# Turning rows into columns by VectorE squares and small transfers instead of TensorE transposes, in a fused GLA and ConvFFN layer

## The chip, the cores and the metric

The kernel runs on one core of a Trainium2 chip. The metric is the time of one execution on the device in microseconds (us). Before the change it was 2142.13 us, the median of three runs (2141.64 to 2144.13). Engines are called as in the profile: PE is TensorE (matmul), PEld its weight load, DVE VectorE, ACT ScalarE, POOL GpSimd, and SP SyncE, which here issues every transfer.

## The reference: what is computed

One layer of a decoder with 2048 tokens of width 1024: gated linear attention (GLA) with 4 heads, then a feed-forward network (FFN) with a causal convolution of width 3. Each of the two is modulated by a vector c, and followed by a residual and a layer norm:

```
def post_norm_residual(x, cs, w_mod, b_mod, ln_gain, ln_bias, sublayer):
    shift, scale, gate = jnp.split((cs @ w_mod + b_mod)[:, None, :], 3, axis=-1)
    y = sublayer(x * (1 + scale) + shift)
    return layer_norm(DN_ALPHA * x + (1 + gate) * y, ln_gain, ln_bias)

x = post_norm_residual(x, cs, mod_w[0, 0], mod_b[0, 0], ln_g[0, 0], ln_b[0, 0], gla)
x = post_norm_residual(x, cs, mod_w[0, 1], mod_b[0, 1], ln_g[0, 1], ln_b[0, 1], ffn)
```

The GLA part is `x @ w_in`, a chunked recurrence with a state per head, a norm per head, a gate, and `@ w_o`. The FFN part is `(silu(conv(u)) * g) @ w_down` with `u, g = split(h @ w_up)`, 2816 channels each. Everything is float32.

## The kernel before

**Number format.** A float32 matrix is split in two parts of PE's fast 32-bit format, high and low: ACT rounds (line 107) and DVE subtracts (line 110). A product is then three matmuls (`mm3`, lines 113 to 115). All matmuls of 512 columns come from there.

**The GLA part.** The tokens are worked on in four blocks of 512 (`tb` = 0 to 3, here the first to the fourth block). Each block goes through 32 units, a unit being one tile of weights of 24 matmuls. Weights come through `unit()`, which asks for the tile three units further on. The split weights are kept in HBM (`wq_d`) and come back from there as 1 MB loads (`hl<-wq_d`, line 136); in the third and fourth blocks all of them do. There are four buffers for them. What isn't a unit's own matmuls (the steps of the heads, the modulation, the gate of the FFN) is hung on unit numbers with `at_unit`, and done in `tick()` between two units. The instructions are then ordered on each engine by a scheduler, within what `order(later, earlier)` asks for. All DMAs leave from one queue on SP, in its order, and eight can be under way: a ninth waits for the first.

**Between GLA and FFN.** At the end of a block `ln1` normalises the rows `z` (128 tokens x 1024) and stores them in `zn_d`. The FFN needs them turned: channels on the partitions, tokens in a row. `ln1_out` does that: for each of 8 column tiles of 128 channels PE transposes four squares of 128x128 into a PSUM tile (line 844), DVE (line 849) or ACT (line 847) applies scale `A2` and shift `B2`, and the tile is stored in `xm2_d`. The second and third blocks do that directly from their rows `z`, behind the block's end. The first block does it in the third one's units 13 to 16, since `A2` and `B2` are not there earlier, with `z` loaded again from `zn_d`. The fourth block does it in the FFN's iterations 3 to 6.

**Also in the third block.** `gate_step` (eight steps, 512 KB load each into a tile of the `raw` pool, line 256; product and sum on DVE, lines 258 and 260) and `gate2` make `G2`, the gate of the FFN: two matmuls with ones (line 268), two additions on DVE (line 269) into `G2t`, stored to `G2_d` (line 888) and loaded later. At the block's end the rows `x` for the residual come in (`z<-in_x`, line 804), and the next block's columns of x (`xraw<-in_xT`, line 386).

**The FFN.** Two halves of 1024 tokens, 22 channel tiles each: 44 iterations. An iteration has seven products of 4 x 3 matmuls (Strassen-like combinations of four quarters, which `x_pre` prepares for the tokens from `xm2_d`), the convolution, and loads of the next pair of weights (`wu`, `wg`, lines 333 and 334). A stage of `hidden @ w_down` and the last norm follow.

Of the kernel before, what the change touches and what calls it, by code (L numbers as in the profile page):

```python
# [8 lines left out]
F32 = mybir.dt.float32  # L9
F32R = mybir.dt.float32r  # L10
U32 = mybir.dt.uint32
AF = mybir.ActivationFunctionType
# [4 lines left out]
P = 128  # L17
D = 1024
S = 2048
KT = D // P  # L20
# [18 lines left out]
def kernel(  # L39
# [46 lines left out]
    def raw_tile(name="raw"):  # L86
        return rawp.tile([P, 1024], F32, tag="raw", name=name)
# [24 lines left out]
    def mm3(po, a, b, first, last, resumed=False):  # L112
        nc.tensor.matmul(po, a[0], b[0], start=first, stop=False, skip_group_check=resumed)  # L113
        nc.tensor.matmul(po, a[0], b[1], start=False, stop=False, skip_group_check=resumed)  # L114
        return nc.tensor.matmul(po, a[1], b[0], start=False, stop=last, skip_group_check=resumed)  # L115
# [81 lines left out]
    ws_d = [dram.tile([P, 2, 512], F32, name=f"ws_d{j}") for j in range(NJ)]  # L197
    xt_d = [[[dram.tile([P, 1024], F32, name=f"xt_d{h}_{i}_{r}") for r in range(2)] for i in range(7)] for h in range(2)]
    wq_d = [dram.tile([P, 2, 1024], F32, name=f"wq_d{n}") for n in range(32)]
    xm2_d = [[dram.tile([P, 2, TB], F32, name=f"xm2_d{t}_{k}") for k in range(4)] for t in range(NTB)]  # L200
    G2_d = dram.tile([P, D], F32, name="G2_d")

# [160 lines left out]
    def at_unit(u, fn, *a):  # L363
        steps.setdefault(u, []).append((fn, a))
# [11 lines left out]
    if True:  # L376
# [288 lines left out]
        def gemm_f(xm):  # L665
            w = unit()
            wv = w.rearrange("p s (k c) -> p s k c", k=KT)
            po = psum("mm", 4)
            for kt in range(KT):
                mm3(po, (wv[:, 0, kt], wv[:, 1, kt]), (xm[kt][:, 0], xm[kt][:, 1]), kt == 0, kt == KT - 1)  # L670
            return po

        def gemm_q(xm, E, tick, pq=None):
# [159 lines left out]
        def ln1_out(tb, zs, prs, by_act=False):  # L833
            for pr in prs:
# [4 lines left out]
                for k in range(2):  # L839
# [9 lines left out]
                        nc.vector.tensor_scalar(xt, pt, A2[:, kt:kt + 1], B2[:, kt:kt + 1], op0=ALU.mult, op1=ALU.add)  # L849
                    store(xm2_d[tb][pr][:, k], xt)  # L850

        def normalise(z, after=None):
            st = smp.tile([P, 2, 6], F32, tag="bst", name="bst")
            for i in range(2):
                bn = nc.vector.bn_stats(st[:, i], z[:, i * 512:i * 512 + 512])
                if after is not None:
                    order(bn, after)
            mv = smp.tile([P, 2], F32, tag="mv", name="mv")
            nc.vector.bn_aggr(mv, st)
            rs = smp.tile([P, 2], F32, tag="rs", name="rs")  # L860
            rsqrt_eps(rs[:, 0:1], mv[:, 1:2])
            nc.gpsimd.tensor_scalar(rs[:, 1:2], mv[:, 0:1], rs[:, 0:1], -1.0, op0=ALU.mult, op1=ALU.mult)
            nc.scalar.activation(z, z, AF.Identity, bias=rs[:, 1:2], scale=rs[:, 0:1])
# [28 lines left out]
        for tb in range(NTB):  # L892
# [18 lines left out]
                        at_unit(b + 6 + n, mod_fin, 1, n // 4)  # L911
                at_unit(b + 22, mod2)
            if tb == 2:
                for pr in range(4):
                    at_unit(b + 13 + pr, ln1_out, 0, None, (pr,))
                for k in range(8):
                    at_unit(b + 14 + k, gate_step, 1, k, gs2)
                at_unit(b + 22, gate2)
# [32 lines left out]
                        Hs[h]["sr"].append(gemm_r(xm, tick))  # L951
            zs = load_z(tb)
            if 0 < tb < NTB - 1:
                at_unit(b + 32 + 2, ln1_out, tb, zs, range(0, 2))
                at_unit(b + 32 + 3, ln1_out, tb, zs, range(2, 4))
            out_proj(tb, 0, gated, zs, tick)
            if last:
                abx.close()
# [21 lines left out]
    if True:  # L980
# [136 lines left out]
        w_h3(W)  # L1117

        nextx, ahead_x = list(PROD), []
        todo = {3 + pr: [(ln1_out, NTB - 1, None, (pr,), True)] for pr in range(4)}  # L1120
        todo |= {9: [(x_pre, 1, 0)], 12: [(x_pre, 1, 1)]}
        G2 = gp.tile([P, D], F32, tag="G", name="G2")
        load(G2, G2_d)
        prev = None
        for n in range(2 * NJ):
# [41 lines left out]
            if prev is not None:  # L1167
                conv_b(prev["h1"], prev["U"], 1, prev["j"])
            pc = st["pc"] = psum("w", 4)
            prod(st, 4, pc, True)  # L1170
            prod(st, 6, pa, False)
            u3, u3i = keep(pa, "u3")
            if prev is not None:
# [245 lines left out]
```

## Time and profile before

| | |
|---|---|
| median of 3 runs | 2142.13 us (2141.64 to 2144.13) |
| profiled execution | 2141.68 us, span 2139.8 us |
| PE busy | 2124.7 us |
| mean granted clock | 0.998 of full speed |
| instructions | 26750 |
| moved by DMA | 529.28 MB, mean 247 GB/s |

The profile is one execution. Its busy times are of instructions; PE's matmuls overlap, so that one of 512 columns shows 0.39 us while the next starts 0.23 us later. The chain is followed back from the last instruction: at each step to what released it or to the instruction ahead of it on its engine. A landing time of a DMA runs from its issue on SP to its semaphore.

### The profile page before, as it was taken

The numbers are of one execution on the slowest core, as the hardware profiler recorded it, in microseconds if no ns is written. First come the engines' busy times: TensorE is split into PE (matmuls) and PEld (weight loads), VectorE is DVE, ScalarE is ACT, GpSimd is POOL, SyncE is SP. The second block draws the span as 40 slices with busy tenths as digits, with TensorE's granted clock in tenths as the row PEclk, the third lists the DMA queues.
The fourth block names the chain that finished last, engine by engine and source line by source line (L and its number), as shares of the span: only waits on it lengthen the run. The fifth ranks groups of instructions, "written<-read, shape, count | busy, mean of one in ns | idle before, by whom it ended". The sixth has DMA issues, their size and how long they took to land.

```text
span 2139.8 us, 26750 instructions
## 1 busy us (share of the span) xinstructions
PE 2124.7 (99%) x9916; PEld 1771.1 (83%) x9916; DVE 1423.3 (67%) x2015; ACT 892.6 (42%) x1356; POOL 115.5 (5%) x258
## 2 busy tenths in 40 slices
PE   9999999999999999999999999999999999999998
PEld 7888888888888888888888888888888888888886
DVE  7876576434743553878777778666666797578557
ACT  4655553433343343544444454333333434344332
POOL 0010100010001000000000000000000000021003
PEclk9999999999999999999999999999999999999999
DMA  8477886664866766777855469878777888577562
GB/s 313 165 259 271 315 325 238 222 249 176 296 228 240 263 243 230 256 260 279 308 191 186 172 214 340 295 247 284 249 263 278 268 309 287 193 243 254 191 204 89
DMA packets 155106, 529.28 MB, mean 247 GB/s; under 512 B 17664, under 2 KB 21888, under 8 KB 134752
## 3 DMA queue, kind: packets, MB, share of 16 engines
q1 hardware_dynamic: 154976, 527.58, 69.9%
q8 instruction: 78, 1.28, 0.2%
q14 instruction: 52, 0.43, 0.1%
HBM read 364.72 MB, written 162.79 MB: 247 GB/s over the span
## 4 chain that ended last, share of the span: by engine, by line
PE 92%; DVE 3%; DMA 3%; ACT 1%; issue 1%; SPq 0%; POOL 0%; POOLq 0%; DVEq 0%; ACTq 0%
PE ps_mm L113 22%; PE ps_mm L115 22%; PE ps_mm L114 22%; PE ps_w L114 8%; PE ps_w L115 8%; PE ps_w L113 8%; DMA raw<-in_wab_dram 2%; DMA xraw<-in_xT_dram 1%; PE ps_w L844 1%; DVE hl L110 1%; PE ps_w L602 1%; PE ps_w L793 1%; ACT hl L107 0%; PE ps_w L529 0%; PE ps_w L528 0%
## 5 line engine op out<-in xcount | busy, mean ns | idle before, releaser
L113 PE MATMUL ps_mm<-xc,hl 128*128 128x512 f32 x704 | 274.3, 390 | 0.0
L114 PE MATMUL ps_mm<-xc,hl 128*128 128x512 f32 x704 | 273.9, 389 | 0.0
L115 PE MATMUL ps_mm<-xc,hl 128*128 128x512 f32 x704 | 273.9, 389 | 0.0
L113 PE MATMUL ps_mm<-xm,hl 128*128 128x512 f32 x496 | 194.9, 393 | 0.5 <-DVE v L110 0.5
L115 PE MATMUL ps_mm<-xm,hl 128*128 128x512 f32 x496 | 193.6, 390 | 0.0
L114 PE MATMUL ps_mm<-xm,hl 128*128 128x512 f32 x496 | 193.5, 390 | 0.0
L113 PEld LDWEIGHTS ps_mm<-xc,hl 128*128 128x128 f32 x704 | 132.1, 188 | 27.5 <-ACT u L1010 0.2
L115 PEld LDWEIGHTS ps_mm<-xc,hl 128*128 128x128 f32 x704 | 132.1, 188 | 27.5
L114 PEld LDWEIGHTS ps_mm<-xc,hl 128*128 128x128 f32 x704 | 132.2, 188 | 27.3
L1024 DVE SCALAR_TENSOR_TENSOR ct<-U,cw_sb,ct 128x512 f32<-128x512 f32 x176 | 131.6, 747 | 22.1 <-ACT ct L1018 20.6
L113 PE MATMUL ps_w<-xc,hl 128*128 128x512 f32 x352 | 136.9, 389 | 0.0
L114 PE MATMUL ps_w<-xc,hl 128*128 128x512 f32 x352 | 136.9, 389 | 0.0
L115 PE MATMUL ps_w<-xc,hl 128*128 128x512 f32 x352 | 136.9, 389 | 0.0
L107 ACT CAST dhl<-raw 128x1024 fp32r<-128x1024 f32 x57 | 60.0, 1053 | 152.3 <-PE ps_mm L115 96.0
L1010 ACT COPY u<-ps_mm 128x512 f32<-128x512 f32 x88 | 51.4, 584 | 154.9 <-PE ps_mm L115 152.9
L107 ACT CAST hl<-raw 128x1024 fp32r<-128x1024 f32 (+1 forms) x73 | 70.0, 965 | 108.8 <-PE ps_mm L115 42.2
L110 DVE TENSOR_TENSOR hl<-raw,hl 128x1024 fp32r<-128x1024 f32 (+1 forms) x73 | 81.0, 1116 | 47.3 <-ACT hl L107 47.1
L110 DVE TENSOR_TENSOR dhl<-raw,dhl 128x1024 fp32r<-128x1024 f32 x57 | 69.5, 1219 | 63.8 <-ACT dhl L107 63.8
L115 PEld LDWEIGHTS ps_mm<-xm,hl 128*128 128x128 f32 x496 | 93.2, 188 | 19.9 <-issue 0.2
L113 PEld LDWEIGHTS ps_mm<-xm,hl 128*128 128x128 f32 x496 | 93.2, 188 | 19.7 <-DVE v L110 1.0
L114 PEld LDWEIGHTS ps_mm<-xm,hl 128*128 128x128 f32 x496 | 93.2, 188 | 18.2 <-issue 0.2
L113 PE MATMUL ps_mm<-dhl 128*128 128x512 f32 x264 | 102.7, 389 | 0.0
(246 smaller groups left out, 4998.0 us busy)
## 6 DMA issues: line engine op xcount, KB each, us to landing
hl<-wq_d SPq DMA_DIRECT2D x82, 1024.0 KB, 5.0
hc_d<-ct SPq DMA_DIRECT2D x154, 256.0 KB, 2.6
raw<-hc_d SPq DMA_DIRECT2D x70, 512.0 KB, 4.2
draw<-wc_d SPq DMA_DIRECT2D x70, 512.0 KB, 4.8
wq_d<-hl SPq DMA_DIRECT2D x32, 1024.0 KB, 5.1
raw<-in_wab_dram SPq DMA_DIRECT2D x46, 512.0 KB, 6.4
wu<-in_wup_dram SPq DMA_DIRECT2D x44, 512.0 KB, 5.6
wg<-in_wup_dram SPq DMA_DIRECT2D x44, 512.0 KB, 4.0
```

The lines of the kernel that those rows point to most:

```text
L107: accs["copy"] = nc.scalar.copy(h, src)
L110: return nc.vector.tensor_tensor(l, src if lsrc is None else lsrc, h.bitcast(F32), op=ALU.subtract)
L113: nc.tensor.matmul(po, a[0], b[0], start=first, stop=False, skip_group_check=resumed)
L114: nc.tensor.matmul(po, a[0], b[1], start=False, stop=False, skip_group_check=resumed)
L115: return nc.tensor.matmul(po, a[1], b[0], start=False, stop=last, skip_group_check=resumed)
L602: nc.tensor.matmul(po, wv[:, a, kt], xm[kt][:, b], start=kt + a + b == 0, stop=kt == KT - 1 and b == 1)
L793: nc.tensor.transpose(pt[:, s * P:s * P + P], on[:, s, e * P:e * P + P], ident)
L844: nc.tensor.transpose(pt[:, t * P:t * P + P], src, ident)
L1010: return t, nc.scalar.copy(t, po)
L1024: nc.vector.scalar_tensor_tensor(ct, U[:, o + i:o + i + 512], cw_sb[:, j, i:i + 1], ct, op0=ALU.mult, op1=ALU.add)
```

## The change

The PE transposes of all four blocks go. Instead:

- `turn_sq`: DVE transposes all squares of 32x32 of a row tile `z` in one instruction (128x1024), into a tile `zt`; a scheduling order puts it behind the last split of weights so far.
- `turn_out`: `zt` is stored in `zt_d`, 512 KB.
- `cols_in`: for one column tile of 128 channels, four transfers of 32 partitions each gather the squares from `zt_d` in the turned places: 16 pieces of 32 numbers (128 B) for each partition, 64 KB a transfer.
- `cols_mod`: a unit (or iteration) later ACT applies `A2` and `B2`, in order behind the last matmul so far (`last_mm`).
- `cols_out`: the tile is stored in `xm2_d`, in order behind the last weight load.

The first and second blocks are turned in the third one, one column tile in each of units 6 to 13 (second block) and 15 to 22 (first block), scaled one unit later and stored one later still. The third and fourth are turned in the FFN's iterations 1 to 8 and 9 to 16, and the second call of `x_pre` for those tokens comes in iterations 16 and 18 instead of 9 and 12.

```
+        def turn_sq(tb, t, z=None):
+            if z is None:
+                z = raw_tile("zr")
+                load(z, zn_d[tb * 4 + t])
+            zt = raw_tile("zt")
+            order(nc.vector.transpose(zt, z), accs["hl"])
+            turned[tb, t] = zt
+
+        def turn_out(tb, t, after):
+            order(store(zt_d[tb][t * P:t * P + P], turned.pop((tb, t))), after())
+
+        def cols_in(tb, kt, tile, after):
+            if kt % 2 == 0:
+                turned[tb, "x", kt // 2] = tile("xt")
+            xt = turned[tb, "x", kt // 2][:, kt % 2 * 512:kt % 2 * 512 + 512]
+            for g in range(4):
+                c = kt * P + g * 32
+                order(load(xt[g * 32:g * 32 + 32].rearrange("i (b j) -> i b j", j=32),
+                           zt_d[tb][:, c:c + 32].rearrange("(b i) j -> i b j", i=32)), after())
+
+        def cols_mod(tb, kt, after):
+            xt = turned[tb, "x", kt // 2][:, kt % 2 * 512:kt % 2 * 512 + 512]
+            order(nc.scalar.activation(xt, xt, AF.Identity, bias=B2[:, kt:kt + 1], scale=A2[:, kt:kt + 1]), after())
+
+        def cols_out(tb, kt, after):
+            xt = turned[tb, "x", kt // 2][:, kt % 2 * 512:kt % 2 * 512 + 512]
+            order(store(xm2_d[tb][kt // 2][:, kt % 2], xt), after())
...
             if tb == 2:
-                for pr in range(4):
-                    at_unit(b + 13 + pr, ln1_out, 0, None, (pr,))
+                for t in range(4):
+                    at_unit(b + 3 + t, turn_sq, 0, t)
+                    at_unit(b + 4 + t, turn_out, 0, t, last_load)
+                for kt in range(KT):
+                    for q, u in ((1, b + 6 + kt), (0, b + 15 + kt)):
+                        at_unit(u, cols_in, q, kt, z_tile if q else raw_tile, last_load)
+                        at_unit(u + 1, cols_mod, q, kt, last_mm)
+                        at_unit(u + 2, cols_out, q, kt, last_load)
...
             if 0 < tb < NTB - 1:
-                at_unit(b + 32 + 2, ln1_out, tb, zs, range(0, 2))
-                at_unit(b + 32 + 3, ln1_out, tb, zs, range(2, 4))
+                if tb == 2 or True:
+                    for t in range(4):
+                        at_unit(b + 32 + 1 + t // 2, turn_sq, tb, t, zs[t])
+                        at_unit(b + 32 + 2 + t // 2, turn_out, tb, t, last_load)
...
-        todo = {3 + pr: [(ln1_out, NTB - 1, None, (pr,), True)] for pr in range(4)}
-        todo |= {9: [(x_pre, 1, 0)], 12: [(x_pre, 1, 1)]}
+        for t in range(4):
+            then(2 + t, turn_sq, NTB - 1, t, zs_last[t])
+            then(3 + t, turn_out, NTB - 1, t, last_h2)
+        for kt in range(KT):
+            for q, n in ((2, 1 + kt), (3, 9 + kt)):
+                then(n, cols_in, q, kt, z_tile, last_h2)
+                then(n + 1, cols_mod, q, kt, last_h2)
+                then(n + 1, cols_out, q, kt, last_h2)
+        then(16, x_pre, 1, 0)
+        then(18, x_pre, 1, 1)
```

Three places show how the instructions stand, each before and now. The first is SP's queue: where the gate's loads (`graw`) leave. Before, the first four leave together with the last weight loads of the second block (`wq_d30`, `wq_d31`; `wq_d0` is the third block's first):

```order
L256 DMA graw_4991<-in_mwg_dram 128x1024 [waits DMAHW0_49,DVE_49]
L256 DMA graw_5053<-in_mwg_dram 128x1024 [waits DMAHW1_49,DVE_49]
L136 DMA hl_3940<-wq_d30_247 128x2048 [waits DMAHW2_49,PE_49]
L256 DMA graw_5111<-in_mwg_dram 128x1024 [waits DMAHW3_49,DVE_49]
L136 DMA hl_3986<-wq_d31_248 128x2048 [waits DMAHW4_49,PE_49]
L256 DMA graw_5147<-in_mwg_dram 128x1024 [waits DMAHW5_49,DVE_49]
L136 DMA hl_4051<-wq_d0_217 128x2048 [waits DMAHW6_49,PE_49]
```

Now the first of them leaves between `wq_d16` and `wq_d17` of the third block, and the queue looks like this for each unit there (`xt` is a column tile, `xm2_d` where it is stored):

```order
L136 DMA hl_4943<-wq_d16_233 128x2048 [waits DMAHW0_49,PE_49]
L882 DMA xm2_d1_3_260<-xt_4888 128x512 [waits DMAHW1_49,Activation_49]
L257 DMA graw_4972<-in_mwg_dram 128x1024 [waits DMAHW2_49]
L136 DMA hl_4975<-wq_d17_234 128x2048 [waits DMAHW3_49,PE_49]
L873 DMA xt_5013<-zt_d0_249 32x16x32 [waits DMAHW4_49]
L873 DMA xt_5013<-zt_d0_249 32x16x32 [waits DMAHW5_49]
L873 DMA xt_5013<-zt_d0_249 32x16x32 [waits DMAHW6_49]
L873 DMA xt_5013<-zt_d0_249 32x16x32 [waits DMAHW7_49]
L882 DMA xm2_d1_3_260<-xt_4888 128x512 [waits DMAHW0_49,Activation_49]
L257 DMA graw_5019<-in_mwg_dram 128x1024 [waits DMAHW1_49]
L136 DMA hl_5022<-wq_d18_235 128x2048 [waits DMAHW2_49,PE_49]
```

So a store that waits for ACT, a gate load and four small transfers now stand between two weight loads.

The second place is SP's queue at the end of the third block, around the store of `G2_d` from `G2t`. Before:

```order
L136 DMA hl_5592<-wq_d26_243 128x2048 [waits DMAHW5_49,DMAHW4_49,PE_49]
L264 DMA G2t_5481<-in_mbg_dram 128x1024 [waits PE_49]
L888 DMA G2_d_265<-G2t_5481 128x1024 [waits DMAHW6_49,DMAHW5_49,DVE_49]
L136 DMA hl_5618<-wq_d27_244 128x2048 [waits DMAHW7_49,DMAHW1_49,PE_49]
L804 DMA z_5580<-in_x_dram 128x1024 [waits DMAHW0_49,Activation_49]
```

Now:

```order
L926 DMA G2_d_269<-G2t_5470 128x1024 [waits DMAHW3_49,DMAHW1_49,DVE_49]
L882 DMA xm2_d0_3_256<-xt_5427 128x512 [waits DMAHW4_49,Activation_49]
L805 DMA z_5571<-in_x_dram 128x1024 [waits DMAHW5_49]
L805 DMA z_5573<-in_x_dram 128x1024 [waits DMAHW6_49]
L805 DMA z_5575<-in_x_dram 128x1024 [waits DMAHW7_49,PE_49,Activation_49]
L805 DMA z_5577<-in_x_dram 128x1024 [waits DMAHW0_49,PE_49,Activation_49]
L136 DMA hl_5583<-wq_d26_243 128x2048
```

The load of `wq_d26` stood ahead of the store of `G2_d` and now stands behind it, a column tile's store and the four loads of `z`.

The third place is DVE at the same time: the additions for `G2t` beside the state updates of the heads (`S32`, `Shl`), and the gated tiles of the third head (`sr`, `gated`). Before:

```order
L269 SCALAR_TENSOR_TENSOR G2t_5481<-ps_w_5483,G2t_5481 128x512
L269 SCALAR_TENSOR_TENSOR G2t_5481<-ps_w_5486,G2t_5481 128x512
L110 TENSOR_TENSOR Shl_5431<-S32_393,Shl_5431 128x256
L756 SCALAR_TENSOR_TENSOR S32_393<-S32_393,el_4874,ps_w_5434 128x256
L795 SCALAR_TENSOR_TENSOR sr_5312<-ps_w_5521,ng_sb_102,sr_5312 128x512
L110 TENSOR_TENSOR Shl_5442<-S32_393,Shl_5442 128x256
L795 SCALAR_TENSOR_TENSOR sr_5376<-ps_w_5530,ng_sb_102,sr_5376 128x512
L756 SCALAR_TENSOR_TENSOR S32_393<-S32_393,el_4874,ps_w_5434 128x256
L110 TENSOR_TENSOR gated_5527<-sr_5312,gated_5527 128x512
L110 TENSOR_TENSOR gated_5536<-sr_5376,gated_5536 128x512
```

Now:

```order
L110 TENSOR_TENSOR Shl_5407<-S32_397,Shl_5407 128x256
L757 SCALAR_TENSOR_TENSOR S32_397<-S32_397,el_4882,ps_w_5410 128x256
L110 TENSOR_TENSOR Shl_5418<-S32_397,Shl_5418 128x256
L757 SCALAR_TENSOR_TENSOR S32_397<-S32_397,el_4882,ps_w_5410 128x256
L796 SCALAR_TENSOR_TENSOR sr_5282<-ps_w_5510,ng_sb_102,sr_5282 128x512
L110 TENSOR_TENSOR Shl_5422<-S32_397,Shl_5422 128x256
L796 SCALAR_TENSOR_TENSOR sr_5352<-ps_w_5519,ng_sb_102,sr_5352 128x512
L110 TENSOR_TENSOR gated_5516<-sr_5282,gated_5516 128x512
L110 TENSOR_TENSOR gated_5525<-sr_5352,gated_5525 128x512
L270 SCALAR_TENSOR_TENSOR G2t_5470<-ps_w_5472,G2t_5470 128x512
L270 SCALAR_TENSOR_TENSOR G2t_5470<-ps_w_5475,G2t_5470 128x512
```

The additions for `G2t` stood ahead of the gated tiles and now stand behind both, and `sr` stands behind one state update more.

## Rows read from the trace of the kernel before

**Rows 1.** The page: busy time by engine (share of the span), and the chain by engine.

```profile
PE 2124.7 (99%) x9916; PEld 1771.1 (83%) x9916; DVE 1423.3 (67%) x2015; ACT 892.6 (42%) x1356; POOL 115.5 (5%) x258
...
PE 92%; DVE 3%; DMA 3%; ACT 1%; issue 1%; SPq 0%; POOL 0%; POOLq 0%; DVEq 0%; ACTq 0%
```

**Rows 2.** Busy us by stretch (third block, FFN), clock, DMA share, GB/s.

```profile
core 0: us, PE busy (x) PEld busy (x) DVE busy (x) ACT busy (x) POOL busy (x), PEclk, DMA share, GB/s
470.00:690.00 220.00, 219.86 (x1112) 184.80 (x1111) 109.85 (x190) 79.96 (x159) 13.86 (x32) 1.00 0.67 237
1010.00:1400.00 390.00, 390.00 (x1723) 322.92 (x1722) 299.61 (x394) 168.78 (x227) 7.94 (x36) 1.00 0.69 244
```

**Rows 3.** The chain in order of time: pieces at line 844 (start, us, instructions).

```profile
473.01 1.75 PE ps_w L844 x16
...
543.81 0.87 PE ps_w L844 x8
...
690.00 1.75 PE ps_w L844 x16
```

**Rows 4.** Groups by line: shapes, count, busy us, mean ns, idle before.

```profile
L849 DVE TENSOR_SCALAR xt<-ps_w,A,B 128x512 f32<-128x512 f32 x24 | 18.3, 803 | 28.7 <-PE ps_w L844 28.7
L281 DVE TENSOR_TENSOR xp<-xp 128x1024 f32<-128x1024 f32 x16 | 19.5, 1222 | 11.9 <-DMA xp<-xm_d 11.8
L847 ACT ACTIVATE xt<-ps_w,B,A 128x512 f32<-128x512 f32 x8 | 5.8, 780 | 0.0
L756 DVE SCALAR_TENSOR_TENSOR S<-S,el,ps_w 128x256 f32<-128x256 f32 x56 | 26.8, 479 | 24.8 <-PE ps_w L115 22.8
```

**Rows 5.** DMA packets, MB, share of 16 engines: from 2.15 to 2.70 us; whole span.

```profile
q1 hardware_dynamic: 131, 0.02, 17.9%
...
q1 hardware_dynamic: 154976, 527.58, 69.9%
```

**Rows 6.** Timeline of PE: first matmul of units 24, 25 and 26, third block.

```profile
617.65 0.40 PE L113 MATMUL ps_mm<-hl,gated 128*128 128x512 f32 x1
...
623.12 0.39 PE L113 MATMUL ps_mm<-hl,gated 128*128 128x512 f32 x1
...
629.36 0.48 PE L113 MATMUL ps_mm<-hl,gated 128*128 128x512 f32 x1
```

**Rows 7.** Who waited for whom: us in total, times, longest.

```profile
SPq L136 <- PE ps_mm L115: 255.3, 54, 10.3
...
SPq L850 <- DVE xt L849: 15.1, 22, 3.0
...
DVE wg L324 <- DMA wg<-in_wup_dram: 7.8, 10, 1.3
...
DVE gacc L260 <- DMA graw<-in_mwg_dram: 5.5, 2, 4.3
```

**Rows 8.** Timeline of DVE near the end of the third block.

```profile
611.43 1.28 DVE L269 SCALAR_TENSOR_TENSOR G2t<-ps_w,G2t 128x512 f32<-128x512 f32 x2
...
617.36 1.28 DVE L110 TENSOR_TENSOR gated<-sr,gated 128x512 fp32r<-128x512 f32 x2
```

**Rows 9.** Timeline of SP's issues there.

```profile
612.74 0.32 SPq L888 DMA_DIRECT2D G_d<-G2t  x1
613.43 0.32 SPq L136 DMA_DIRECT2D hl<-wq_d  x1
613.84 1.59 SPq L804 DMA_DIRECT2D z<-in_x_dram  x3
```

**Rows 10.** DMA issues: count, KB each, median us to landing.

```profile
hl<-wq_d SPq DMA_DIRECT2D x82, 1024.0 KB, 5.0
...
z<-in_x_dram SPq DMA_DIRECT2D x16, 512.0 KB, 7.3
...
zc<-zn_d SPq DMA_DIRECT2D x32, 128.0 KB, 3.5
```

More of the change, by code (lines that the diff above doesn't have):

```diff
@@ L199 @@
     wq_d = [dram.tile([P, 2, 1024], F32, name=f"wq_d{n}") for n in range(32)]
+    zt_d = [dram.tile([TB, D], F32, name=f"zt_d{t}") for t in range(NTB)]
     xm2_d = [[dram.tile([P, 2, TB], F32, name=f"xm2_d{t}_{k}") for k in range(4)] for t in range(NTB)]
@@ L669, in gemm_f @@
             for kt in range(KT):
-                mm3(po, (wv[:, 0, kt], wv[:, 1, kt]), (xm[kt][:, 0], xm[kt][:, 1]), kt == 0, kt == KT - 1)
+                accs["mm"] = mm3(po, (wv[:, 0, kt], wv[:, 1, kt]), (xm[kt][:, 0], xm[kt][:, 1]), kt == 0, kt == KT - 1)
             return po
@@ L850, in ln1_out, with last_load, last_mm @@
                     store(xm2_d[tb][pr][:, k], xt)
+        turned = {}
+        def turn_sq(tb, t, z=None):
[21 more added lines that the diff above has]
+            order(store(xm2_d[tb][kt // 2][:, kt % 2], xt), after())
+        def last_load():
+            return stream_loads[-1]
+        def last_mm():
+            return accs["mm"]
         def normalise(z, after=None):
@@ L953 @@
             if 0 < tb < NTB - 1:
-                at_unit(b + 32 + 2, ln1_out, tb, zs, range(0, 2))
-                at_unit(b + 32 + 3, ln1_out, tb, zs, range(2, 4))
+                if tb == 2 or True:
+                    for t in range(4):
+                        at_unit(b + 32 + 1 + t // 2, turn_sq, tb, t, zs[t])
+                        at_unit(b + 32 + 2 + t // 2, turn_out, tb, t, last_load)
+                else:
+                    at_unit(b + 32 + 2, ln1_out, tb, zs, range(0, 2))
+                    at_unit(b + 32 + 3, ln1_out, tb, zs, range(2, 4))
             out_proj(tb, 0, gated, zs, tick)
@@ L1119, with then, last_h2 @@
         nextx, ahead_x = list(PROD), []
-        todo = {3 + pr: [(ln1_out, NTB - 1, None, (pr,), True)] for pr in range(4)}
-        todo |= {9: [(x_pre, 1, 0)], 12: [(x_pre, 1, 1)]}
+        todo = {}
+        def then(n, f, *a):
+            todo.setdefault(n, []).append((f, *a))
+        def last_h2():
+            return accs["h2"]
+        for t in range(4):
[8 more added lines that the diff above has]
+        then(18, x_pre, 1, 1)
         G2 = gp.tile([P, D], F32, tag="G", name="G2")
@@ L1169 @@
             pc = st["pc"] = psum("w", 4)
-            prod(st, 4, pc, True)
+            accs["h2"] = prod(st, 4, pc, True)
             prod(st, 6, pa, False)
```

## The prediction

> **What bounds the kernel now.** I read the busy line of the page and the chain that ended last, then the busy times by stretch, the waits of VectorE (DVE) and of the load queue (SP), and the timeline around the one place that decides most. TensorE (PE) is busy 99% of the span and holds 92% of the chain [rows 1]; in the stretches that the change touches it is idle for 0.14 of 220 us and for nothing in 390 us, while the 16 DMA engines are used 67 to 69% there [rows 2]. So an instruction taken from PE there is worth its whole length, as long as nothing that PE needs comes later; and whatever comes later is paid in full. The question is only how much cover the feeders have.
>
> **What is taken from PE.** 128 transposes of 128x128 go: four times 16 in 1.75 us and eight times 8 in 0.87 us, each as one piece of the chain [rows 3]: 4 x 1.75 + 8 x 0.87 = 14.0 us. All of them are on the chain, so this is the whole gain: -14.0 us.
>
> **What is added beside PE.** DVE loses 24 scalings of 0.80 us (19.3 us) and gets 16 square transposes of 128x1024. No row has that operation; the nearest, a 128x1024 subtraction, takes 1.22 us [rows 4]. That or twice that is 19.5 or 39 us on an engine that is 67% busy [rows 1]; I take 1.22, and even twice is hidden. ScalarE (ACT) scales all 32 tiles instead of 8: 24 more at 0.78 us [rows 4] are 18.7 us on an engine 42% busy. Neither sum is on the path; the order in which these instructions stand is, see below.
>
> SP gets 128 small transfers, 16 stores of transposed rows and 4 loads, and loses 32 loads. A small transfer fetches 64 KB as 512 packets of 128 B. The nearest row of that packet size is the first load of 16 KB: 131 packets, nearly all of 128 B, used 17.9% of 16 engines for 0.55 us [rows 5], 0.179 x 16 x 0.55 / 131 = 12 ns each. The far end is the mean packet of the run, 0.699 x 16 x 2139.8 / 154976 = 154 ns [rows 5], of about 3.4 KB. I take 12 ns, the row of the same size; but there the source was contiguous and here every packet is 4 KB behind the last, so dearer is open. At 12 ns a column tile (2048 packets) costs 2048 x 12 / 16 = 1.5 us of all engines. In the third block 16 tiles go through 18 units. A unit is (690.00 - 473.01) / 32 = 6.78 us on average [rows 3], so that is 122 us, of which 67% or 82 us are used already [rows 2]. With 16 x 1.5 = 24 us, and 8 stores of 512 KB at 353 GB/s (247 GB/s at 69.9% use) for 12 us, it is 118 of 122: it just fits, and takes away all slack. In the FFN an iteration is 84 matmuls at 0.228 us (24 from 617.65 to 623.12) [rows 6], 19.1 us, used 69% (13.2 us); 1.5 and some 1 more fit.
>
> **What moves: the cover of the loads in the third block.** In the kernel before, SP mostly stands waiting for PE to free a weight buffer (255 us in 54 waits) [rows 7]: each load leaves as soon as it may, some three units ahead of its use. The store of a column tile, by contrast, waited little for DVE (15.1 us in 22 waits). Now, in each of 16 units, a store of a scaled tile, which waits for ACT, stands ahead of a gate load, a weight load and four small transfers (first pair of pieces of the order). ACT scales a tile only behind the last matmul of its unit, so everything queued behind the store leaves about one unit before its use and no longer three. What this costs, place by place:
>
> (a) The store of G2 (second pair of pieces). Before, the 27th weight load (wq_d26) stood ahead of it. Now it stands behind it, behind a store and four loads of z. And on DVE the two additions that make G2t now stand behind both gated tiles (third pair). The gated tiles of that head end at 617.36 + 1.28 = 618.6 [rows 8], with the additions (1.28) 619.9. SP then issues the two stores and four z (0.32 each; three z took 1.59) [rows 9], and has 0.5 + 0.25 + 4 x 0.5 MB queued ahead of the 1 MB. 3.9 million bytes at 353 GB/s are 11.1 us, and the tail of a 1 MB load is 2.0 us (5.0 to landing, 3.0 of it bytes) [rows 10]: it lands near 633. PE wants it at 629.36 [rows 6]. Cost 3.8 us.
>
> (b) The first gate step stands ahead of the four subtractions on v on DVE, before and now. Before, its load came a block earlier; now one unit ahead. A 512 KB load in a crowded queue lands after 7.3 us (z) [rows 10]; with 0.75 for the step that is 8.0 against one unit of 5.45 [rows 6]: 2.6 us, and PE's four banks wait for v.
>
> (c) DVE's order: the product for a head's gated tiles stands behind one state update more than before (third pair), and the fourth head's key product behind two. An update is 0.48 on DVE [rows 4], with its rounding on ACT and remainder on DVE about 1.3 us, an estimate. Three of them 3.9 us. The last gate step, loaded as late, 1 us.
>
> (d) The loads of the next block's x move from ahead of wq_d23 to behind wq_d27, and early in the fourth block a weight load falls behind eight transfers of x_pre. Each by the reckoning of (b) 2.6 us, together 5.2.
>
> Sum of the third block and the start of the fourth 16.5 us. If the cover holds after all it is 0; if every one of 18 units pays as in (b), 47.
>
> **The FFN.** 16 iterations each put four small transfers and a store that waits for ACT ahead of the next pair of weight loads. The second of the pair (wg) has no cover left as it is: DVE waited for it 7.8 us in 10 of 44 iterations, 0.78 each [rows 7]. I take one such wait in each of the 16: 12.5 us. Below: 0. Above: four issues in each at the pace of the z loads (1.59 / 3 = 0.53) [rows 9], 34 us.
>
> **Sum.** The profiled execution took 2141.68 us (span 2139.8), 0.45 below the median of 2142.13. 2141.7 - 14.0 + 16.5 + 12.5 = 2156.7, so 2157. The bounds: 2141.7 - 14.0 = 2128 to 2141.7 - 14.0 + 47 + 34 = 2209, at 12 ns a packet.
>
> **Rivals.**
> 1. The cover holds: ACT, 42% busy, scales early, SP does not stand at the stores, PE just loses its transposes. 2128. For it: before, the store of a tile cost SP only 15.1 us, and the gate loads made DVE wait only twice (5.5 us in all) [rows 7]. Against it: the G2 store's new place is fixed by the order, and (a) needs no guess on ACT.
> 2. The waits come to about half of mine and eat the gain: 2142. For it: 0.78 us of DVE's wait need not reach PE, which has products queued.
> 3. The small packets are dear, and the DMA engines become the bound of the third block, on the slower side. It decides from where 82 + 12 + 16 tiles pass 122 us: 1.75 us a tile, 14 ns a packet, so little above my price. At 36 ns (three times) a tile is 4.6 us: 82 + 12 + 74 = 168, 46 over; the FFN still fits (13.2 + 4.6 + 1 of 19.1). 2141.7 - 14 + 46 + 12.5 = 2186. At 154 ns it would be hundreds of us. For it: a stride of 4 KB in the source, which no row has with such packets. Against it: the 1 KB pieces of zn, at the same stride, land after 3.5 us for 128 KB [rows 10].
>
> The Trainium skill, "DMA: Bandwidth & Descriptors", section "Rules for kernel authors", advises against transposing by a plain DMA with a rearranged access pattern and gives a factor of 19. No run here shows it yet. Taken on a tile of 256 KB (0.74 us at 353 GB/s) it would be 14 us a tile or 110 ns a packet, and with the DMA engines as bound (third block 82 + 12 + 225 - 122 = 197 over, FFN 16 x (13.2 + 14.1 + 1 - 19.1) = 147) about 2470. I give it 0.03 of its own: the squares are already turned on DVE, so that 128 B stay together, where element by element would fit the rule better.
>
> 4. The change not doing what it says (PE still transposing) is excluded by the order: the 128 transposes are gone.
>
> **How the numbers follow.** Forecast 0.58, with its own range of 2146 to 2174 (half to one and a half times the 29 us of waits); rival 1 0.10; rival 2 0.10; rival 3 0.19; the factor of 19 0.03. A measurement of this kernel can tell 0.2% from no change, 4.3 us: 2137.4 to 2146. Faster is rival 1 (0.10); same is most of rival 2 and the edge of the forecast (0.10); slower the rest, 0.80. For 8 in 10 the range leaves out rival 1 and the upper half of rival 3: 2139 to 2198.
>
> **What would show it.** Right: no transposes of z on PE; PE idle for some 15 us between the start of the third block and the start of the fourth, with its longest wait at the 27th weight load of the third block; DVE waiting for gate loads and wg; SP waiting at the stores for ACT; packets of 128 B near 12 ns. Wrong: PE still without idle time there (rival 1); DMA use above 95% through the third block (rival 3). If the idle time of PE is mainly elsewhere, the places are wrong though the sum be right.

## The result and the profile after

The changed kernel takes 2163.3 us (median of 4 runs, 2162.6 to 2163.8) against 2143.1 us for the kernel before on the same chip: a ratio of 1.0095, 95% interval 1.0083 to 1.0108. It is slower by 20 us. The profiled execution has a span of 2161.4 us, 21.6 more than before, and a mean granted clock of 0.995 (0.998 before).

The page after. The rows are busy time by engine, packets by size, the load queue's share of 16 engines, and the chain by engine.

```profile
PE 2121.3 (98%) x9788; PEld 1762.5 (82%) x9788; DVE 1425.3 (66%) x2007; ACT 907.8 (42%) x1380; POOL 113.8 (5%) x258
...
DMA packets 220962, 543.96 MB, mean 252 GB/s; under 512 B 85056, under 2 KB 85184, under 8 KB 200608
...
q1 hardware_dynamic: 220832, 542.27, 72.1%
...
PE 86%; DMA 5%; DVE 5%; ACT 2%; issue 1%; SPq 0%; POOL 0%; POOLq 0%; DVEq 0%; ACTq 0%
```

PE's busy time went down by 3.4 us only [rows 1], although 128 transposes of 14.0 us [rows 3] are gone. PE's share of the chain fell from 92 to 86%; DVE and DMA rose to 5% each.

Busy time by stretch: us, PE, PEld, DVE, ACT, POOL, clock, DMA share, GB/s. The three rows cover the third block, the fourth and the start of the FFN, and the FFN up to the last tile.

```profile
470.00:700.00 230.00, 212.90 (x1015) 175.73 (x1013) 104.22 (x177) 87.82 (x170) 12.54 (x32) 0.97 0.77 257
700.00:920.00 220.00, 217.85 (x1063) 183.73 (x1062) 115.09 (x180) 90.34 (x166) 11.28 (x22) 0.99 0.69 254
920.00:1400.00 480.00, 473.73 (x2084) 390.56 (x2083) 373.72 (x493) 217.34 (x296) 13.87 (x53) 1.00 0.75 259
```

PE, which stood 0.2 us in all in these stretches before (0.14 of it in the third block [rows 2]), now stands 17.1 us in the third block, 2.15 between there and the FFN, and 6.3 in the FFN. What it waited for most from 470 to 1400 us (total, times, longest; `hl` is a tile of split weights, `v`, `KI`, `S` and `on` are a head's values, key product, state and normed output, `u` is a product of the FFN):

```profile
PE ps_mm L113 <- DMA hl<-wq_d: 8.5, 2, 6.4
PE ps_mm L113 <- DVE v L110: 4.4, 1, 4.4
PE ps_mm L113 <- ACT hl L107: 3.3, 2, 2.2
PE ps_w L714 <- DVE KI L698: 3.2, 1, 3.2
PE ps_mm L113 <- ACT u L1059: 2.8, 1, 2.8
PE ps_w L794 <- DVE S L757: 1.5, 1, 1.5
PE ps_w L794 <- ACT on L786: 0.8, 1, 0.8
```

And four of the pieces of the chain that are no work of PE (start, us, what): a gate load, the 27th weight load of the third block, a weight load at the start of the fourth, and one of the FFN's.

```profile
548.10 6.60 DMA graw<-in_mwg_dram
...
633.77 9.57 DMA hl<-wq_d
...
719.15 6.58 DMA hl<-wq_d
991.30 4.42 DMA wu<-in_wup_dram
```

The longest stop is the 27th weight load, as forecast. It has a second price, which the prediction did not have. PE's timeline around it, and the granted clock in stretches of 2 us:

```profile
636.61 0.39 PE L115 MATMUL ps_mm<-hl,gated 128*128 128x512 f32 x1
643.38 0.79 PE L113 MATMUL ps_mm<-hl,gated 128*128 128x512 f32 x1 [6.38 <-DMA hl<-wq_d]
...
648.57 0.39 PE L113 MATMUL ps_mm<-hl,gated 128*128 128x512 f32 x1
```

```profile
640.00:642.00 2.00, 0.00 (x0) 0.00 (x0) 0.00 (x0) 0.00 (x0) 0.00 (x0) 0.90 0.97 387
...
644.00:646.00 2.00, 2.00 (x6) 1.61 (x5) 0.00 (x0) 0.00 (x0) 0.00 (x0) 0.50 0.97 406
```

PE stands for 6.38 us. Then the granted clock is 0.50, which is 1.2 of 2.4 GHz, and a matmul starts every 0.43 us where it started every 0.23; from 648.57 it is back to 0.23. The 12 matmuls between lost 12 x 0.2 = 2.4 us. The Trainium skill, "TensorE: Matmul & The Clock Gate", section "Part 1: The HAM clock gate (the "warmup" mystery)", says that a gate passes half of the array's clock or all of it, by how busy the engine has been; the trace agrees, with 0.50 behind 6.38 us of standing.

So the account of the profiled span is: transposes -14.0; PE standing 17.1 + 2.15 + 6.3 - 0.2 (before) = +25.3; and PE's busy time 2121.3 - (2124.7 - 14.0) = +10.6. The sum is +21.9 of 21.6 us. The 10.6 are a remainder and not all of it is the clock. The granted clock, 0.97 over 230 us and 0.99 over 220, can have cost about 0.03 x 230 + 0.01 x 220 = 9 us at the most. And two kernels below that have no transposes and few stops (e_no_turn and e_order_wide) have PE busy for 2113.4 and 2113.3 us, where 2124.7 - 14.0 would be 2110.7. So some 8 us (2121.3 - 2113.3) come with the stops, most of them work at the lower clock; the other 2.6 are a part of the 14.0 that does not arrive, and why it doesn't is open.

### The profile page after: what moved, and what is told of

Read it like the earlier page. It is cut to its first block, busy times and chain, and to the rows that moved or that the text cites. A ratio compares the mean times of both kernels' runs of the same rounds, so it can differ in the third digit from the quotient of the medians.

```text
span 2161.4 us, 26611 instructions
## 1 busy us (share of the span) xinstructions
PE 2121.3 (98%) x9788; PEld 1762.5 (82%) x9788; DVE 1425.3 (66%) x2007; ACT 907.8 (42%) x1380; POOL 113.8 (5%) x258
## 4 chain that ended last, share of the span: by engine, by line
PE 86%; DMA 5%; DVE 5%; ACT 2%; issue 1%; SPq 0%; POOL 0%; POOLq 0%; DVEq 0%; ACTq 0%
PE ps_mm L113 21%; PE ps_mm L115 21%; PE ps_mm L114 20%; PE ps_w L114 7%; PE ps_w L115 7%; PE ps_w L113 7%; DMA raw<-in_wab_dram 3%; DMA xraw<-in_xT_dram 1%; DVE hl L110 1%; DMA hl<-wq_d 1%; DMA graw<-in_mwg_dram 1%; ACT hl L107 1%; PE ps_w L794 0%; DVE sr L796 0%; DVE az L514 0%
## 5 line engine op out<-in xcount | busy, mean ns | idle before, releaser
L113 PE MATMUL ps_mm<-hl,gated 128*128 128x512 f32 x256 | 101.5, 396 | 6.5 <-DMA hl<-wq_d 6.4
L1067 ACT ACTIVATE ct<-U,cb_sb,cw_sb 128x512 f32<-128x512 f32 x88 | 71.6, 814 | 83.2 <-DVE U L325 83.2
```

What stands on the lines that cost most here:

```text
L1067: nc.scalar.activation(ct, U[:, o + 2:o + 514], AF.Identity, bias=cb_sb[:, j:j + 1], scale=cw_sb[:, j, 2:3])
```

## The experiments

A time is the median of 4 to 11 runs, a ratio is against the kernel before on the same chip, with its 95% interval. The changed kernel's own is 1.0095.

**1. The gain alone (e_no_turn).** Scaling reads the rows in place of the transposed tile:

```
-                        nc.tensor.transpose(pt[:, t * P:t * P + P], src, ident)
...
+                    pt = z[:, k * 512:k * 512 + 512] if zs is None else zs[kt // 2][:, k * 512:k * 512 + 512]
```

> The kernel before with its 128 transposes of 128x128 taken away and nothing in their place: the scaling reads the rows z directly, so the turning itself is left out. It measures the gain term alone. Theory (the transposes stand whole on the chain): 2143.1 - 14.0 = 2129, no PE waits of more than 1 us in the third block. Rival (other work flows into the gaps, or PE waits where it used to transpose): a gain under 7 us, 2136 or more. The changed kernel's PE busy time fell by only 3.4 us; if the granted clock explains the rest, the busy time of PE falls here by 14 us at a clock that stays at 0.998.

Measured: 2132.0 us, ratio 0.9954 (0.9941 to 0.9966), so -10.6 us. PE's busy time fell by 11.3, to 2113.4. Most of the term of 14.0 is real; some 3 us of it do not arrive. The clock is 0.997, and in the third block PE has one wait of 0.6 us, so the clock after stops does not explain all of the busy time that the changed kernel did not save. Both theories are off by 3 to 4 us, the first the nearer.

**2 and 3. One half each (e_ffn_only, e_gla_only).** The diff of the change with only its FFN part, or only its third-block part.

> Only the third and fourth blocks (turned in the FFN) go by squares; the first and second are transposed by PE as before. Gain of 64 transposes -7.0 us. Theory after the trace of the changed kernel: PE waits in the FFN are 6.3 us at three places, so 2143.1 - 7.0 + 6.3 = 2142.4, within 0.2% of before. The prediction's own term (one 0.78 us wait of wg in each of 16 iterations, 12.5): 2148.6. Rival (the FFN waits are the backlog of stores and loads that the third block left behind, and go with it): 2136.

> Only the first and second blocks (turned in the third block) go by squares; the third and fourth are transposed by PE as before. Gain -7.0 us. Theory (loads late behind stores on SP, then PE waits, then a lower granted clock): PE waits of 19 us between the start of the third and the start of the fourth block, and some 9 us through the clock at its lower level: 2143.1 - 7.0 + 19 + 9 = 2164, as slow as the whole change. By the prediction's term (16.5, no clock term): 2153. If the third block is not where the loss is: under 2145.

Measured: 2146.8 us, ratio 1.0017 (1.0009 to 1.0026), and 2161.6, ratio 1.0087 (1.0073 to 1.0100). The third block's part alone loses nearly all; by stretch, the FFN part first and the third-block part second:

```profile
920.00:1400.00 480.00, 473.56 (x2076) 390.20 (x2075) 368.71 (x484) 213.74 (x292) 10.14 (x46) 1.00 0.76 261
```

```profile
470.00:700.00 230.00, 212.18 (x1000) 175.13 (x999) 99.87 (x173) 87.92 (x170) 12.52 (x32) 0.96 0.76 255
```

Each half keeps its own loss: 6.4 us of standing in the FFN without the other's work, 17.8 in the third block at a clock of 0.96. So the FFN's waits are no backlog of the third block. The FFN part alone is 4 us above its theory, although PE stands as that said: its PE is busy 2122.3 us, 4.6 more than 2124.7 - 7.0. The time of the prediction's own term, 2148.6, is nearer, but its 12.5 us of standing are not there.

**4. Long runs in place of 128 B (e_wide).**

```
-                           zt_d[tb][:, c:c + 32].rearrange("(b i) j -> i b j", i=32)), after())
+                           zt_d[tb][c // 2:c // 2 + 16].rearrange("a (i c) -> (a i) c", i=2)), after())
```

> The changed kernel with the same number of small transfers and the same bytes, but each reads 2 KB runs in place of 128 B pieces, so that the numbers land in wrong places (the turning is left out); the order of issues on SP stays nearly the same. Per tile it takes (1.5 - 0.7) = 0.8 us off the DMA engines, 12 us in the third block. Theory (the order of SP's queue, loads behind stores that wait for ACT): nearly nothing, 2156 to 2163, with the waits for graw and wq_d still there. Rival (small packets fill the DMA engines and the loads land late because of them): most of the 30 us of waits and clock goes, 2135 to 2145.

Measured: 2135.9 us, ratio 0.9967 (0.9954 to 0.9979). By its expectation this is rival 3, the small packets, and my theory was out by 20 us. I took it for that, and the next run was to show how it grows with the number of packets.

**5. Half the packets (e_256).** The same with pieces of 256 B.

> The changed kernel with the same small transfers and bytes, but 256 packets of 256 B in each in place of 512 of 128 B, from wrong places (the turning is left out). With 2 KB runs nearly all PE waits had gone (2135.9). Theory now (the packets fill the DMA engines in bursts, the loads then lose the cover that their place behind the stores leaves them): half the packets take about half of what they add, 1.5 us a tile down to some 1.1, and since the loss begins only where the engines are full, most of it goes: 2138 to 2146. Rival (what counts is that a run is shorter than some length): as slow as the changed kernel, 2157 to 2163.

Measured: 2160.6 us, ratio 1.0089 (1.0076 to 1.0102): half the packets, and no less loss. That is the range of its rival, that any short run costs as much; runs 9 and 10 decide on that. By stretch, the changed kernel and then this one:

```profile
470.00:540.00 70.00, 69.11 (x361) 58.57 (x360) 33.75 (x61) 33.68 (x71) 3.32 (x7) 1.00 0.78 247
540.00:600.00 60.00, 52.45 (x248) 43.75 (x247) 27.22 (x45) 18.25 (x33) 0.52 (x3) 0.94 0.84 255
```

```profile
470.00:540.00 70.00, 69.11 (x361) 58.55 (x360) 33.66 (x61) 33.00 (x70) 2.75 (x4) 1.00 0.72 251
540.00:600.00 60.00, 52.28 (x252) 43.50 (x251) 27.42 (x47) 19.65 (x35) 1.07 (x6) 0.94 0.77 256
```

The DMA engines are used 0.06 to 0.07 less, and PE stands the same 0.89 and 7.6 to 7.7 us. So their use does not make the loss. I then compared the rows of all engines. The 256 B kernel has them in the order of the changed kernel, row for row. The 2 KB kernel does not: the scheduler, which orders by durations of its own for each transfer, gives some 140 lines of difference on DVE, 90 on ACT, 190 on PE and 50 on SP. Run 4 had changed two things.

**6 to 8. Where the queue's work stands (e_act_queue, e_gate_early, e_spread).**

```
-            order(store(xm2_d[tb][kt // 2][:, kt % 2], xt), after())
+            order(nc.scalar.dma_start(xm2_d[tb][kt // 2][:, kt % 2], xt), after())
```

```
-                    at_unit(b + 14 + k, gate_step, 1, k, gs2)
-                at_unit(b + 22, gate2)
+                    at_unit(b + k // 2, gate_step, 1, k, gs2)
+                at_unit(b + 5, gate2)
```

```
+            if tb == 1:
+                for t in range(4):
+                    at_unit(b + 24 + t, turn_sq, 0, t)
+                    at_unit(b + 25 + t, turn_out, 0, t, last_load)
...
+                for m in range(2 * KT):
+                    q, kt, u = m // KT, m % KT, b + 5 * m // 4
```

> The changed kernel with the stores of the scaled tiles issued by ACT on its own queue, so that no load on SP stands behind a store that waits for ACT; packets unchanged. The prediction's theory (place behind the stores): most of the 19 us of PE waits of the third block go, 2140 to 2148. Theory now (packets fill the DMA engines; the place only sets how much is lost): a part goes, 2148 to 2157. Rival (packets alone, place without effect): 2163.

> The changed kernel with the eight gate steps in units 0 to 3 of the third block (two in each) and the end of the gate at unit 5, so that the gate's 4 MB no longer leave among the small transfers of units 15 to 22, and the store of G2 no longer stands ahead of the 27th weight load. Theory: the two long gate waits (6.6 and 6.1 us on the chain), the 9.6 us piece at the 27th load and the clock behind them go, and the FFN's 6 us stay: 2145 to 2150. Rival (4 MB more in the first five units, where the DMA engines are used 0.99 to 1.00 already between 490 and 510 us): the waits move there, 2158 to 2166.

> The changed kernel with the first block's rows turned and stored at the end of the second block, and the 16 tiles of the third block in its units 0 to 18 (one in 1.25 units) ahead of most gate loads, in place of units 6 to 13 and 15 to 22. The same transfers in all. Theory (bursts of the DMA engines): with 4 MB of rows out of the third block's first units and the gate loads beside few tiles, half or more of the third block's 28 us goes: 2143 to 2152; the store of G2 still waits for the gated tiles. Rival (the place behind the stores decides, and that is the same here): 2158 to 2165.

Measured: 2151.6 (1.0044, 1.0032 to 1.0056), 2163.3 (1.0096, 1.0083 to 1.0109) and 2163.2 us (1.0101, 1.0088 to 1.0114). Only the first gains, 12 us, in the range of the theory that packets fill the DMA engines; the other two lie in the ranges of their rivals. In the second the waits moved into the first units, as its rival said, and in the third PE stands 10 us between 540 and 600 us. But the scheduler reordered the engines in each of them too, so that none tells place from order. The next three hold the order.

**9 to 11. Order and packets apart (e_order_wide, e_packets_wide, e_order_act).** The program is traced twice; the order of the first pass is imposed on the second, instruction by instruction, on PE, DVE, ACT and SP:

```
+            for name in seq:
+                i = traced.get(name)
...
+                if i.engine in last:
+                    tc.add_manual_dep(i, last[i.engine], ...)
+                last[i.engine] = name
...
+    _, _, seq = build(True, [])         # order of the 2 KB runs
+    nc, arrays, _ = build(False, seq)   # transfers of 128 B
```

That is e_order_wide. In e_packets_wide the two flags are swapped; e_order_act has the stores of run 6 as well, in both passes.

> The changed kernel with its own transfers of 128 B packets, but with the instructions on TensorE, VectorE, ScalarE and SP held in the order that they had in the run with 2 KB runs (that run had changed both: the scheduler, which takes transfers of long runs for shorter, had also ordered 142 rows of VectorE, 93 of ScalarE, 185 of TensorE and 49 of SP otherwise). Nothing is left out. Theory A (the order of the instructions on the engines makes the loss): 2136 to 2143, the waits of the third block gone. Theory B (the small packets make it): 2157 to 2163. Half and half: near 2149. The 256 B run, whose order was the changed kernel's to the row and which lost as much (2160.6), speaks for A.

> The reverse: 2 KB runs (wrong places, the turning left out) in the order of the changed kernel on every engine. Theory A (order): 2155 to 2163, the same waits at the gate loads and at the 27th weight load. Theory B (packets): 2135 to 2142. Half and half: near 2149.

> The changed kernel with its own transfers, ordered as the scheduler orders it when it takes the small transfers for 2 KB runs, and with the tiles' stores issued by ACT on its own queue as in the run that brought 12 us. A version that may beat both kernels. If order and place behind the stores each make a part: 2132 to 2138. If order alone decides: as e_order_wide. If packets decide: as the ACT queue run, 2148 to 2155.

| | order of the changed kernel | order of run 4 |
|---|---|---|
| 128 B packets | 2163.3, ratio 1.0095 (1.0083 to 1.0108) | 2133.4, ratio 0.9955 (0.9941 to 0.9969) |
| 2 KB runs | 2160.7, ratio 1.0088 (1.0074 to 1.0103) | 2135.9, ratio 0.9967 (0.9954 to 0.9979) |

The order moves the time by 25 to 30 us, the packets by no more than 3, once up and once down, with intervals that overlap. Theory A holds; e_order_wide is even below its range. What is shown is the order of PE, DVE, ACT and SP together; no run moved one engine's whole order alone. With the stores on ACT's queue as well the kernel takes 2131.7 us, ratio 0.9947 (0.9934 to 0.9960); its interval overlaps that of e_order_wide. Both do the whole computation, and beat the kernel before by about 0.5% and the changed one by 1.4 to 1.5%. By stretch, 2 KB runs in the changed kernel's order, and then 128 B packets in run 4's order:

```profile
470.00:700.00 230.00, 213.46 (x1018) 176.28 (x1017) 104.36 (x177) 87.98 (x170) 12.54 (x32) 0.97 0.71 257
...
920.00:1400.00 480.00, 475.69 (x2093) 392.07 (x2092) 374.43 (x495) 216.32 (x294) 13.69 (x52) 1.00 0.72 262
```

```profile
470.00:540.00 70.00, 70.00 (x364) 59.89 (x363) 31.20 (x58) 32.91 (x69) 2.75 (x4) 1.00 0.95 292
540.00:600.00 60.00, 60.00 (x303) 50.93 (x302) 32.46 (x52) 23.50 (x42) 1.40 (x6) 1.00 0.91 278
470.00:700.00 230.00, 227.59 (x1105) 188.54 (x1104) 114.83 (x192) 93.31 (x178) 12.85 (x32) 1.00 0.86 289
...
920.00:1400.00 480.00, 480.00 (x2118) 397.32 (x2117) 372.17 (x492) 216.20 (x294) 14.63 (x46) 1.00 0.77 265
```

The second is the one to look at: the DMA engines are used 0.95 and 0.91 of the time, with the small packets, and PE does not stand there at all. SP stands at the tiles' stores there too. First the changed kernel, then e_order_wide:

```profile
SPq L882 <- ACT xt L878: 65.6, 15, 7.0
```

```profile
SPq L890 <- ACT xt L886: 44.9, 11, 7.6
```

**12. One engine's part (e_act_scale).** Only the places of scalings among ACT's instructions are moved, to where run 4 has them; all else keeps the changed kernel's order. By the traces 14 of them, in the third block, stand earlier, and 5, in the FFN, stand later, which its expectation does not say:

```
+        for n in act(alt):
+            if n in SCALED:
+                held.append(n)
+            else:
+                before[n], held = held, []
```

> The changed kernel with one edit: 17 scalings of tiles on ACT stand earlier among ACT's other instructions, each ahead of the one that it stood ahead of in the order that took 2133.4 us (in the first places that is ahead of KI and Shl roundings, of sr, or of the two steps of E). TensorE, VectorE and SP keep the changed kernel's order row for row, packets and transfers too. Theory (a store on SP waits for a scaling that stands late on ACT, and the loads behind it lose their cover): the gate waits (v 4.4 and KI 3.2 us, and the clock behind them) go; the store of G2 still waits for DVE's additions, which stand behind the gated tiles (6.4 us and the clock behind it), and the FFN keeps a part of its 6 us: 2147 to 2154. If ACT's places are the whole cause: 2133 to 2140. Rival (VectorE's order, gate steps ahead of v and of the state updates, makes the loss): 2158 to 2163.

Measured: 2163.7 us, ratio 1.0094 (1.0077 to 1.0111), no gain in the whole time. One of PE's waits (as above), and two stretches:

```profile
PE ps_w L719 <- DVE KI L703: 3.1, 1, 3.1
```

```profile
540.00:600.00 60.00, 56.83 (x272) 47.72 (x272) 30.72 (x51) 23.72 (x43) 1.07 (x6) 0.94 0.80 236
...
920.00:1400.00 480.00, 471.48 (x2060) 388.32 (x2059) 370.10 (x489) 215.25 (x294) 13.70 (x52) 0.99 0.74 257
```

The wait for v (4.4 us) has gone, as its theory said, but KI's and the 27th load's (6.0) stay. The unchanged total hides a gain and two losses. From 540 to 600 us PE stands 3.2 us and not 7.6; matched matmul by matmul, the profiled execution makes up 7.0 us against the changed kernel between the end of the second block and the fourth (a matmul at 469.62 there stands at 475.01 here, and one at 759.70 at 758.12). In the FFN, where five scalings stand later, PE stands 8.5 us and not 6.3, at a clock of 0.99. And in the first 470 us, ahead of any moved instruction, it stands 10.9 us and not 6.4 in this execution, the slowest of the four. So late scalings make the wait for v and carry several us of the third block's loss, but not most of it. Whether DVE's order, PE's or the rest of ACT's weighs more was not tried.

**Where order becomes time.** Two places can be read in the traces of the changed kernel and e_order_wide (in which L886 is L878, and so on by 4 to 8 lines). At the end of the third block ACT has these orders (`gated` is the rounding of a gated tile, `on` and `sq` are the next head's norm):

```
changed kernel                           e_order_wide
on<-ps_w                                 gated<-sr
sq,ss<-on x2                             Shl<-S32
on<-ps_w                                 gated<-sr
sq,ss<-on x2                             xt<-xt,B2,A2
gated<-sr                                on<-ps_w
gated<-sr                                Shl<-S32
on<-on,ss x4                             sq,ss<-on x2
```

In the changed kernel the two roundings of `gated` stand behind the fourth head's norm, which waits for PE. ACT, DVE and SP of the changed kernel (start, us, how many):

```profile
624.25 0.59 ACT L780 COPY on<-ps_w 128x512 f32<-128x512 f32 x1 [2.00 <-PE ps_w L115]
...
627.38 1.12 ACT L107 CAST gated<-sr 128x512 fp32r<-128x512 f32 x2
```

```profile
622.71 0.74 DVE L796 SCALAR_TENSOR_TENSOR sr<-ps_w,ng_sb,sr 128x512 f32<-128x512 f32 x1
628.02 1.29 DVE L110 TENSOR_TENSOR gated<-sr,gated 128x512 fp32r<-128x512 f32 x2 [4.57 <-ACT gated L107]
629.23 1.28 DVE L270 SCALAR_TENSOR_TENSOR G2t<-ps_w,G2t 128x512 f32<-128x512 f32 x2
```

```profile
544.56 0.34 SPq L882 DMA_DIRECT2D xm_d<-xt  x1
...
630.54 0.32 SPq L926 DMA_DIRECT2D G_d<-G2t  x1
...
633.77 0.45 SPq L136 DMA_DIRECT2D hl<-wq_d  x1
```

And e_order_wide:

```profile
611.73 0.68 DVE L114 TENSOR_TENSOR gated<-sr,gated 128x512 fp32r<-128x512 f32 x1
```

```profile
615.64 0.32 SPq L934 DMA_DIRECT2D G_d<-G2t  x1
...
617.79 0.43 SPq L140 DMA_DIRECT2D hl<-wq_d  x1
624.75 0.33 SPq L809 DMA_DIRECT2D z<-in_x_dram  x1
```

```profile
626.11 0.50 PE L117 MATMUL ps_mm<-hl,gated 128*128 128x512 f32 x1 [1.74 <-DMA hl<-wq_d]
```

`sr` is done by 623.5, but ACT rounds it at 627.38, so the gated tiles come at 628.02 after 4.57 us of DVE waiting, the additions of G2 at 629.23, the store at 630.54, and the 27th load at 633.77, for PE's want at 637.0. In the other order the gated tiles stand ahead, and the load leaves at 617.79. Most of these 16 us is no gain at this place: PE there is ahead as a whole, wants the load at 624.4, 12.6 us sooner, and still stands 1.74 us. The load leaves 3.4 us earlier against PE's want, and takes 8.3 us where it took 9.6. Nor is it ACT's order alone: SP's differs here too. The fourth load of `z`, which could leave only at 624.75, stands behind the weight load; up to the store of G2 SP's order in the third block is the same in both kernels.

The second place is the key product of the fourth head on DVE (`KI<-KI,el`), and the transposes of `KI` on PE that wait for it, in the changed kernel and then in e_order_wide:

```profile
585.24 0.69 DVE L698 TENSOR_TENSOR KI<-KI,el 128x512 f32<-128x512 f32 x1
...
586.08 0.63 PE L714 MATMUL ps_w<-ident,KI 128*128 128x128 f32 x4 [3.17 <-DVE KI L698]
```

```profile
579.33 0.68 DVE L702 TENSOR_TENSOR KI<-KI,el 128x512 f32<-128x512 f32 x1
...
583.02 0.60 PE L718 MATMUL ps_w<-ident,KI 128*128 128x128 f32 x4
```

In the first it stands behind both state updates; in the second behind one, and starts 5.9 us earlier. But PE is 5 to 6 us ahead there by then (the same matmul starts at 571.71 and at 566.69, a later one at 580.48 and at 574.21), so that for PE KI comes hardly sooner. By these rows it is PE's own order that ends the wait of 3.2 us: in e_order_wide 24 matmuls more (`ps_mm<-xm,hl`, a unit) stand ahead of these transposes, and PE reaches them 3.0 us after KI is there. No run changes PE's order or DVE's alone, so this is read and not tested.

## Why the prediction was right, and where not

The forecast was 2157 in a range of 2139 to 2198, slower with 0.80; the time is 2163.3. Its sum held, its reason in part, and that the sum came so near is partly luck. (Half to one and a half times its 29 us of waits would be 2142 to 2171 and not 2146 to 2174; the time lies in both.)

- **Transposes, -14.0.** They left the chain. Taken alone they gave 10.6.
- **Beside PE.** The sizes were right: the transpose of squares, which no row had, takes what the subtraction took, 1.23 us and not twice that. Where the work stands does reach the path: a scaling on ACT is in the chain at (b).

```profile
L861 DVE STREAM_TRANSPOSE zt<-z 128x1024 f32<-128x1024 f32 x12 | 14.8, 1231 | 3.1 <-ACT z L901 3.0
```

- **12 ns a packet.** Right. The load queue used 0.721 x 16 x 2161.4 - 0.699 x 16 x 2139.8 = 1003 engine-us more [rows 5]; 8.4 of its 14.7 MB more are small packets, the other 6.3 MB at 353 GB/s take 285, and (1003 - 285) / 65,536 = 11 ns, an estimate. The Trainium skill, "DMA: Bandwidth & Descriptors", section "Rules for kernel authors", would have made it 110 ns by its factor of 19, as the prediction estimated; no run here shows that for pieces of 128 B. Rival 3 fell in two ways: the packets are cheap, and "it just fits" is harmless, since in e_order_wide PE runs without a stop at 0.91 to 0.95 of the DMA engines.
- **(a) The 27th load, 3.8.** The right place, the right chain, the longest stop: 6.4 us. The step took the gated tiles' end from the trace of before, 618.6; it was 629.3. Of these 10.7 us, 7.6 are PE's own delay up to there (its want moved from 629.36 to 637.0), and some 3 the place of the roundings behind the norm on ACT.
- **(b) The first gate load ahead of v, 2.6.** The place is right (4.4 us), its reason in part wrong. A load one unit ahead is enough: in e_order_wide it stands in the same place of SP's queue, and PE does not wait. It came late because SP stood at a store until 544.56 (above) for a scaling that ACT did behind the steps of E, and that is what run 12 took away:

```profile
543.73 1.50 ACT L878 ACTIVATE xt<-xt,B,A 128x512 f32<-128x512 f32 x2
```

- **(c) DVE's order, 4.9.** Near in size: KI 3.2, S 1.5, the gate 0.4, 5.1 in all. At KI PE's order counts as well, as shown above. A wait of 0.8 for ACT's `on` was not foreseen.
- **(d) The fourth block's start, 5.2.** 2.1 us. (a) to (d) with `on` are 18.8 where 16.5 were forecast.
- **FFN, 12.5.** The step that failed. One wg wait for each of 16 iterations was taken; DVE waited 9.3 us for wg in 11 iterations, 1.5 more than before [rows 7], and PE stood 6.3 us in three places:

```profile
DVE wg L325 <- DMA wg<-in_wup_dram: 9.3, 11, 1.3
```

- **The clock.** Missing from the sum: some 8 us of busy time behind the stops, most of it work at the lower clock. FFN too high by 6, and this too low by 8, the transposes' missing 2.6 and the 2.3 of (a) to (d) leave 7 us between sum and time: errors that nearly made up for each other.

The prediction's main picture, that everything queued behind a store loses its cover, is not what carries the loss. It holds at v, where a late scaling held up a store and the gate load behind it; but SP stands 45 us at those stores in a kernel without the loss. What the runs show in its place is the order in which the scheduler put the heads' own steps, on PE, DVE, ACT and SP taken together; which engine's order weighs most stays open. (a) and (c), which were read from the order, are of that kind and held, (b), (d) and the FFN, which were argued from the cover, did not hold as argued. Rival 1, the cover that holds, was no wrong picture of the queue: e_order_wide comes within 6 us of its 2128.

## What to carry to other kernels

Where a scheduler sets the order, an edit to a transfer also edits every engine's order: compare the rows of all engines before calling an effect by the edit's name, and hold the order fixed to tell the two apart. An experiment that changes a shape (2 KB for 128 B) is two experiments. When the same instruction starts earlier in one kernel than in another, take off first by how much PE is ahead there. And a stop of PE can cost more than its length: the work at the lower clock behind it.

## What the runs showed of the hardware

- 65,536 packets of 128 B at a stride of 4 KB cost about 11 ns of an engine each (by the sum above), and DMA engines used 0.91 to 0.95 for 130 us did not delay PE in e_order_wide.
- DVE transposes the 32x32 squares of a 128x1024 tile in 1.23 us, as long as it takes to subtract one (1.22 [rows 4]).
- After 6.38 us of standing the granted clock was 0.50 and the next 12 matmuls started 0.43 us apart; in the whole run some 8 us of busy time came with 25 us of standing.
